# One kernel, one change: the small matmuls of a first loop put one by one between its wide ones

## The chip, the cores and the metric

The kernel runs on one core of one Trainium2 chip. The metric is the device time of one execution in microseconds (us), lower is better. TensorE is called PE in the profile, VectorE DVE, ScalarE ACT, GpSimd POOL; SP is the engine whose queue issues the DMAs.

## The reference

One layer of a decoder trunk on x of 2048 rows by 1024 columns, with one conditioning vector c: a modulated norm, a gated short convolution, a residual and a last norm.

```python
def reference(x, c, ..., final_g, l0_ada_w, l0_ada_b, l0_w_in, l0_conv_w, l0_conv_b, l0_w_out):
    shift, scale, gate = split(silu(c) @ ada_w + ada_b, 3)
    h = rmsnorm(x) * (1.0 + scale) + shift            # (2048, 1024)
    u, gc, gb, z = split(h @ w_in, 4)                 # w_in: 1024 x 8192
    conv = causal_conv3(gc * u, conv_w)               # per channel, width 3
    y = (gb * (conv + conv_b) * silu(z)) @ w_out      # w_out: 2048 x 1024
    return rmsnorm(x + gate * y, final_g)
```

## The kernel before, in words

**The big product.** h @ w_in is done by a scheme with seven products in place of eight (the "Pair" class): h and w_in are cut into 2x2 blocks, and sums of blocks are multiplied. Each operand is split in two parts, a rounded one (hi) made by ACT and the rest (lo) made by DVE, and each product is three passes of PE: lo x hi, hi x hi, hi x lo (`PASSES`). A product of one pair is 12 wide matmuls (128x512 out): four contraction tiles by three passes. The operands on the side of h are called by the number of the product: 1 and 2 are the blocks of h of the first 512 rows; 5, 6, 7 and 4 are the sums T1, T2, T3 and T4; 3 is a block of the second 512 rows (`b22`).

**The first loop.** Nothing of h exists at the start. Rows come in chunks of 512 (`x0`, then `x1`): four tiles each, loaded, squared and summed by ACT (`norm_x`, line 110, whose scratch tile `sq` comes from the pool `raw` of four buffers), a root on POOL, scaled by DVE (line 133). For each of the eight contraction tiles k the loop makes shift and scale of that tile, of silu(c) and the weights `ada` (line 181: part of the sum on DVE; line 192: the other part and the sum over partitions by matmuls of one column on PE, here "mods"; lines 193 and 194 copy the two results out), transposes the four tiles of x0 on PE (line 139), applies shift and scale on ACT (`make_h`, line 144), splits, and runs 18 wide matmuls (line 471: products 1 and 2 of six pairs that are kept in six of the eight PSUM banks). Then it does the four transposes and `make_h` for x1, and DVE makes T1 and T2. So a step is, on PE: 8 transposes, 10 mod matmuls, 18 wide. Weights of a step (`raw`, loaded by `load_early`, split to `we`) come through the same pool `raw`.

**After the loop** come the small conv parameters (`make_conv`, whose 16 tiny transposes are line 237), then T3, T4 and all the splits of operands 7, 5, 4 and 3, and then 436 products (line 294), pair by pair, in the order 1, 6, 7, 5, 2, 4, 3; a few side jobs (`make_second`: the same for the other 1024 rows) run between them. At the end y @ w_out (line 646) and the last norm.

**Order.** Each engine works its own queue in order. The order in a queue is set by a scheduler when the program is built, from the order of the code and from when a tile's buffer comes free; DMAs are issued in order by SP. The lines where work stands in the code are printed below, with what calls them.

Of the kernel before, what the change touches and what calls it, by code (L numbers as in the profile page):

```python
# [13 lines left out]
P = 128  # L14
# [4 lines left out]
def trunk_kernel(ctx: ExitStack, tc: tile.TileContext, x, c, final_g, ada_w, ada_b,  # L19
# [47 lines left out]
    def raw(name="raw"):  # L67
        return rawp.tile([P, D], F32, name=name, tag="raw")
# [52 lines left out]
    def load_x(ci):  # L121

        xs = []
        for t in range(ci * ST, (ci + 1) * ST):
            a = op("xn", F32)
            nc.sync.dma_start(a.rearrange("p h n -> p (h n)"), x[t * P:(t + 1) * P, :])
            xs.append(a)
        return xs

    def norm_x(a):  # L130

        scratch = raw("sq").rearrange("p (h n) -> p h n", h=2)
        nc.vector.tensor_scalar_mul(a, a, rstd(square_sum(a, scratch)))

    def turn_x(xns, k):

        tp = bank()
        for t, a in enumerate(xns):
            nc.tensor.transpose(tp[:, t * P:(t + 1) * P], a[:, k // KH, k % KH * P:(k % KH + 1) * P], ident)  # L139
        return tp  # L140

    def make_h(a, tp, k):

# [16 lines left out]
    def mod_start(k):  # L160

        m = sp.tile([P, 2, MC], F32, name="mod", tag="sp")
        nc.vector.memset(m, 0.0)
        nc.sync.dma_start(m[0:1], ada_b.rearrange("(o t n) -> o t n", o=1, t=3)[:, 0:2, k * P:k * P + MC])
        return m

# [28 lines left out]

    def make_gate():

# [133 lines left out]
    class Pair:  # L331


        def __init__(self, hf, g):
            self.g, self.mx = g, mixer(hf, g)
            self.ps = {}

        def target(self, p):

# [26 lines left out]
        def take(self, p, ps):  # L366
            mx, b = self.mx, self.g % 2
            if p == 1:
                self.keep_p1(el("u")[:, :CH])
            elif p == 6:  # L370
                nc.vector.tensor_add(self.u, ps, self.u)
            elif p == 7:
# [7 lines left out]
            elif p == 5:  # L380
# [29 lines left out]
    warm_up(early[-1].ps["A"], ones, 28)  # L410
    x0 = load_x(0)
    mods = [mod_start(k) for k in range(0, KD, 2)]

    def load_early(k):
        r = raw()[:, :2 * EU * P]
# [2 lines left out]
                              w_view[:, k, q, 0:EU, :])  # L418
        return r

    def split_early(r):
        hi, lo = [wp.tile([P, 2 * EU * P], F32R, name="we", tag="w") for _ in range(2)]
        split(r, hi, lo, nc.vector)
        return hi, lo

    def half_block(n):

        ts = [op("hr", F32) for _ in range(2)]
        return [ts[k // 2][:, k % 2] for k in range(KH)]

    ada = {0: load_ada(0)}
    we = {k: load_early(k) for k in range(2)}
    for a in x0:
        norm_x(a)
    ada[2] = load_ada(2)
    x1 = load_x(1)
    h0, h1 = [], []
    bops = {1: [], 2: [], 6: []}
    keep = {}

    def kept(e, name):
# [5 lines left out]
        keep["n"] = keep.get("n", 0) + 1  # L447
        return keep["t"][:, 1 - keep["n"] % 2]

    t2 = []  # L450
    for k in range(KD):
        if k % 2 == 0:
            mod_sum(mods[k // 2], ada[k][:2])
            if 0 < k < KD - 2:
                ada[k + 2] = load_ada(k + 2)
            for i in (k + 2, k + 3):
                if i < KD:
                    we[i] = load_early(i)
        mod_turn(mods[k // 2], ada[k // 2 * 2][2:], k)
        tp = turn_x(x0, k)  # L460
        if k % KH == 0:
            h0 += half_block("h0")
        make_h(h0[k], tp, k)
        t = op("b")
        nc.vector.tensor_copy(t[:, 0], h0[k])  # L465
        nc.vector.tensor_sub(t[:, 1], h0[k], t[:, 0].bitcast(F32))
        bops[1 if k < KH else 2].append(t)
        w = split_early(we.pop(k))
        for n, (i, m) in enumerate(PASSES):
            for e, pr in enumerate(early):  # L470
                nc.tensor.matmul(pr.ps["A"], lhsT=w[i][:, e * P:(e + 1) * P], rhs=t[:, m],  # L471
                                 start=k == 0 and n == 0, stop=k % KH == KH - 1 and n == 2, skip_group_check=True)
        if k == KH - 1:
            for e, pr in enumerate(early):
                pr.keep_p1(kept(e, "p1"), nc.scalar.copy if e % 2 else nc.vector.tensor_copy)
        if k == 0:
            for a in x1:
                norm_x(a)
        if k % KH == 0:
            h1 += half_block("h1")  # L480
        make_h(h1[k], turn_x(x1, k), k)
        if k < KH:
            nc.vector.tensor_sub(h0[k], h1[k], h0[k])
        else:
            t2.append(sp.tile([P, CH], F32, name="t2", tag="sp"))
            nc.vector.tensor_sub(t2[-1], h1[k], h0[k - KH])
            bops[6].append(split_op(t2[-1]))
    for e, pr in enumerate(early):
        pr.take_c11(kept(e, "c11"))
    make_conv()  # L490
    t1, b21, b12, b22 = h0[:KH], h0[KH:], h1[:KH], h1[KH:]
    for k in range(KH):
        nc.vector.tensor_sub(b12[k], b22[k], b12[k])
    bops[7] = [split_op(a) for a in b12]
    bops[5] = [split_op(a) for a in t1]
    for k in range(KH):
        nc.vector.tensor_sub(b21[k], b21[k], t2[k])
    bops[4] = [split_op(a) for a in b21]
    bops[3] = [split_op(a) for a in b22]


    def make_second():
# [58 lines left out]
            yield  # L561


    work = [(0, g + d, p) for g in range(0, 2 * EU, 2) for p in ORDER if p not in (1, 2) for d in range(2)]
# [144 lines left out]
```

## Time and profile before

| | |
|---|---|
| median of 3 runs (lowest to highest) | 1677.51 us (1677.24 to 1679.03) |
| the profiled execution's own time | 1677.48 us |
| its span, first to last instruction | 1675.7 us |
| mean granted clock of PE, 1.0 = full | 0.982 |
| PE busy | 1635.2 us, 98% |
| DVE busy | 1039.4 us, 62% |
| ACT busy | 529.1 us, 32% |

The time of a run is the span and 1.78 us around it. The granted clock is 1.0 at 2.4 GHz and 0.5 at 1.2 GHz; values between are averages. In the profile a float32 matmul of the mods (128x1) is two records of weight load and matmul, a wide matmul and a transpose are one.

### The profile page before, as it was taken

The page shows a single profiled execution, that of the slowest core. Times are in us where ns is not written, and L with a number is a line of the kernel's source. Part 1 is how long each engine was busy: PE and PEld are TensorE (multiplying, and loading weights), DVE is VectorE, ACT ScalarE, POOL GpSimd, SP SyncE. Part 2 cuts the span into 40 slices and gives each one's busy share as a digit, 9 for nine tenths or more (in the row PEclk, how much of TensorE's full clock was granted, in tenths as well). Part 3 has the DMA queues.
Part 4 walks back from the last instruction along what each step waited for, and adds up shares of the span by engine and source line. Part 5 has one row for each costly group of instructions (what it writes and reads, how often), then busy time and mean ns, then how long its engine had stood idle before and what let it go on. Part 6 is the DMA issues. An engine that isn't in the chain of part 4 may idle for free.

```text
span 1675.7 us, 19351 instructions
## 1 busy us (share of the span) xinstructions
PE 1635.2 (98%) x7276; PEld 1351.4 (81%) x7276; DVE 1039.4 (62%) x1602; ACT 529.1 (32%) x881; POOL 150.9 (9%) x230
## 2 busy tenths in 40 slices
PE   6969999999999999999999999999999999999997
PEld 6758888888888878888888888888888888888886
DVE  5568786767787886666766766666666642233331
ACT  4342344443433333333333333333333421111110
POOL 2000120100011011001000000010100100000000
PEclk7879999999999999999999999999999999999999
DMA  8323334334555532752222222222224643333320
GB/s 286 117 82 93 103 95 129 97 121 149 165 176 176 177 125 82 284 181 63 70 76 76 64 63 63 78 74 69 64 70 122 199 144 101 101 101 101 98 85 31
DMA packets 213103, 190.58 MB, mean 114 GB/s; under 512 B 7425, under 2 KB 181513, under 8 KB 213010
## 3 DMA queue, kind: packets, MB, share of 16 engines
q1 hardware_dynamic: 213010, 189.35, 35.9%
q8 instruction: 57, 0.93, 0.2%
q14 instruction: 36, 0.29, 0.1%
HBM read 144.75 MB, written 44.56 MB: 113 GB/s over the span
## 4 chain that ended last, share of the span: by engine, by line
PE 77%; issue 16%; DVE 4%; DMA 2%; POOL 1%; ACT 0%; SPq 0%; DVEq 0%; POOLq 0%; ACTq 0%
PE ps L294 67%; PE ps L646 5%; PE ps L471 2%; PE ps L192 1%; DMA raw<-in_l_w_in_dram 1%; DVE b L148 1%; PE ps L139 1%; DVE w L148 1%; DMA xn<-in_x_dram 0%; POOL rs L118 0%; DVE gate_m L210 0%; POOL t L317 0%; DMA ada<-in_l_ada_w_dram 0%; DVE mod L181 0%; ACT hr L144 0%
## 5 line engine op out<-in xcount | busy, mean ns | idle before, releaser
L294 PE MATMUL ps<-b,w 128*128 128x512 f32 x5232 | 1194.2, 390 | 14.8 <-DVE w L148 13.7
L294 PEld LDWEIGHTS ps<-b,w 128*128 128x128 f32 x5232 | 982.4, 188 | 219.8 <-issue 14.1
L147 ACT CAST w<-raw 128x512 fp32r<-128x512 f32 x244 | 151.7, 622 | 383.0 <-PE ps L294 302.5
L147 ACT CAST w<-s 128x512 fp32r<-128x512 f32 x192 | 118.7, 619 | 200.2 <-PE ps L294 191.5
L646 PE MATMUL ps<-wo,ye 128*128 128x512 f32 x768 | 180.7, 394 | 0.0
L646 PE MATMUL ps<-wo,yw 128*128 128x512 f32 x768 | 176.9, 389 | 0.0
L148 DVE TENSOR_TENSOR w<-s,w 128x512 fp32r<-128x512 f32 x192 | 132.8, 692 | 68.6 <-ACT w L147 68.2
L646 PEld LDWEIGHTS ps<-wo,ye 128*128 128x128 f32 x768 | 144.2, 188 | 34.0
L148 DVE TENSOR_TENSOR w<-raw,w 128x512 fp32r<-128x512 f32 x244 | 167.2, 686 | 4.8 <-ACT w L147 4.6
L646 PEld LDWEIGHTS ps<-wo,yw 128*128 128x128 f32 x768 | 144.2, 188 | 30.3
L659 DVE TENSOR_TENSOR a<-ps,gate 128x512 f32<-128x512 f32 x32 | 22.0, 691 | 191.8 <-PE ps L646 191.7
L316 DVE SCALAR_TENSOR_TENSOR t<-v,cpar,t 128x512 f32<-128x512 f32 x128 | 95.6, 747 | 40.1 <-ACT t L314 39.2
L110 ACT ACTIVATE sq<-xa 128x1024 f32<-128x1024 f32 x16 | 17.0, 1061 | 273.8 <-DVE xa L660 251.2
L312 POOL COPY v<-v 128x2 f32<-128x2 f32 x32 | 20.0, 625 | 740.1 <-DVE v L364 618.9
L318 DVE TENSOR_TENSOR t<-t,gb 128x512 f32<-128x512 f32 x64 | 44.3, 692 | 53.0 <-POOL t L317 53.0
L269 DVE TENSOR_TENSOR s<-raw 128x512 f32<-128x512 f32 x64 | 44.0, 688 | 48.3 <-DMA raw<-in_l_w_in_dram 48.2
L393 DVE TENSOR_TENSOR u<-ps,u 128x512 f32<-128x512 f32 x58 | 39.9, 688 | 39.8 <-PE ps L294 39.8
L353 ACT COPY u<-ps 128x512 f32<-128x512 f32 x58 | 34.0, 586 | 91.9 <-PE ps L294 91.9
L314 ACT ACTIVATE t<-v,cpar 128x512 f32<-128x512 f32 x64 | 52.0, 815 | 5.0 <-DVE v L400 4.3
L471 PE MATMUL ps<-b,we 128*128 128x512 f32 x144 | 45.5, 483 | 5.7 <-DVE b L465 5.7
L317 POOL TENSOR_TENSOR t<-t,sz 128x512 f32<-128x512 f32 x29 | 40.2, 1387 | 115.6 <-DVE t L316 95.2
L317 POOL TENSOR_TENSOR t<-t,u 128x512 f32<-128x512 f32 x29 | 39.4, 1359 | 118.5 <-issue 79.1
(97 smaller groups left out, 948.5 us busy)
## 6 DMA issues: line engine op xcount, KB each, us to landing
raw<-in_l_w_in_dram SPq DMA_DIRECT2D x128, 512.0 KB, 4.3
y_d<-t SPq DMA_DIRECT2D x64, 256.0 KB, 2.4
yr<-y_d SPq DMA_DIRECT2D x32, 512.0 KB, 4.7
op_d<-b SPq DMA_DIRECT2D x28, 512.0 KB, 3.5
b<-op_d SPq DMA_DIRECT2D x28, 512.0 KB, 9.5
xn<-in_x_dram SPq DMA_DIRECT2D x16, 512.0 KB, 4.8
ada<-in_l_ada_w_dram SPq DMA_DIRECT2D x32, 256.0 KB, 4.7
raw<-in_l_w_out_dram SPq DMA_DIRECT2D x16, 512.0 KB, 4.7
```

What stands on the lines that cost most here:

```text
L147: nc.scalar.copy(hi, src)
L148: eng.tensor_sub(lo, src, hi.bitcast(F32))
L269: nc.vector.tensor_add(d, a21, a22)
L294: nc.tensor.matmul(ps, lhsT=w[:, i, k * P:(k + 1) * P], rhs=b[k][:, m], start=first and k == 0 and n == 0, stop=k == KH - 1 and n == 2, sk ...
L314: nc.scalar.activation(t, v[:, 2:], AF.Identity, bias=cpar[:, j, 3:4], scale=cpar[:, j, 2:3])
L316: nc.vector.scalar_tensor_tensor(t, v[:, w:CH + w], cpar[:, j, w:w + 1], t, ALU.mult, ALU.add)
L317: nc.gpsimd.tensor_mul(t, t, self.sz[ci])
L318: nc.vector.tensor_mul(t, t, self.gb[ci])
L353: (eng or nc.scalar.copy)(a, self.ps["A"])
L393: nc.vector.tensor_add(self.u, ps, self.u)
L471: nc.tensor.matmul(pr.ps["A"], lhsT=w[i][:, e * P:(e + 1) * P], rhs=t[:, m], start=k == 0 and n == 0, stop=k % KH == KH - 1 and n == 2, sk ...
L646: nc.tensor.matmul(ps, lhsT=a, rhs=b, start=j == 0 and n == 0, stop=j == NJ - 1 and n == 2)
```

## The change

Five things change, all but one of them in the first loop and around it.

1. **The loop is staggered.** In step k the transposes of tile k+1 (x0), from k = 4 on those of two tiles of x1, and the mods of tile k+2 are generators of which one matmul is taken after each wide one. Before the loop come the mods of tiles 0 and 1 and the transposes of tile 0. Two more rows of warm-up matmuls (16 and 8) stand there.
2. **More of the modulation on DVE.** Of four tiles of `ada` DVE sums three, not two (two for the first pair of tiles): 22 sums of 128x512, not 16, and 20 + 36 mod matmuls on PE, not 80.
3. **The sums T3, T4 and the split of `b22`** leave the gap ahead of the products and come after the first operands: T3 ahead of product 0, T4 behind the first, `b22` behind the third. The six first pairs take the products in the order 6, 5, 7, 4, 3. T1 and T2 are split in the loop.
4. **Loads.** Four weight tiles `raw` are asked for before `norm_x` (two before), `x1` in the loop, the conv parameters at the start (in another pool).
5. **The rounded part of h** is made by ACT (line 150), not by DVE (line 465), and the `mod` tiles are cleared by POOL.

```diff
-        nc.vector.memset(m, 0.0)
+        nc.gpsimd.memset(m, 0.0)
...
                 nc.tensor.matmul(ps[:, t:t + 1], lhsT=a, rhs=b, start=n == 0, stop=n == len(todo) - 1)
+                if (t, n) != (1, len(todo) - 1):
+                    yield
...
-            r = raw("conv")
+            r = op("conv", F32).rearrange("p h n -> p (h n)")
...
+    ON_DVE = {0: KD // AR // 2}
+    def sum_mod(k):
+        mod_sum(mods[k], ada[k][:ON_DVE.get(k, KD // AR - 1)])
...
+    def turn_h0(k):
+        tp = bank()
+        for t in range(ST):
+            turn_one(tp, x0, k, t)
+            if t < ST - 1:
+                yield
+        if k % KH == 0:
+            h0.extend(half_block())
+        make_h(h0[k], tp, k)
+        bops[1 if k < KH else 2].append(split_op(h0[k]))
+        split_early(k)
+        yield
...
+    for k in range(2):
+        we[k] = load_early(k)
+    ada[2] = load_ada(2)
+    for k in range(2, 4):
+        we[k] = load_early(k)
+    for a in x0:
+        norm_x(a)
+    sum_mod(0)
+    warm_up(early[-1].ps["A"], ones, 16)
+    for k in range(2):
+        run_all(turn_mod(k))
+    run_all(turn_h0(0))
...
+        jobs = []
+        if k + 1 < KD:
+            jobs.append(turn_h0(k + 1))
+        if k >= KH:
+            jobs += [turn_h1(2 * (k - KH) + i) for i in range(2)]
+        if k + 2 < KD:
+            jobs.append(turn_mod(k + 2))
...
         for n, (i, m) in enumerate(PASSES):
             for e, pr in enumerate(early):
-                nc.tensor.matmul(pr.ps["A"], lhsT=w[i][:, e * P:(e + 1) * P], rhs=t[:, m],
+                nc.tensor.matmul(pr.ps["A"], lhsT=wk[k][i][:, e * P:(e + 1) * P], rhs=b[:, m],
                                  start=k == 0 and n == 0, stop=k % KH == KH - 1 and n == 2, skip_group_check=True)
+                while jobs and next(jobs[0], StopIteration) is StopIteration:
+                    jobs.pop(0)
...
+    make_t3()
     second = {}
     for n, (hf, g, p) in enumerate(work):
         prepare(n + AHEAD)
+        if n == 1:
+            make_t4()
+        if n == 3:
+            make_b22()
```

What the scheduler made of it, engine by engine. First **PE, in the middle of the loop** (`xn` is a tile of x, `ada` and `mod` belong to the mods, `b` and `we` are the operands of a wide matmul). Before, one whole step:

```order
L139 MATMUL ps<-ident,xn 128x128 x8
L192 MATMUL ps<-sc,ada 128x1 x4
L192 MATMUL ps<-ones,mod 128x1
L192 MATMUL ps<-sc,ada 128x1 x4
L192 MATMUL ps<-ones,mod 128x1
L471 MATMUL ps<-b,we 128x512 x18
```

and now, a piece where the fifth step passes into the sixth:

```order
L195 MATMUL ps<-sc,ada 128x1
L542 MATMUL ps<-b,we 128x512
L195 MATMUL ps<-ones,mod 128x1
L542 MATMUL ps<-b,we 128x512
L143 MATMUL ps<-ident,xn 128x128
L542 MATMUL ps<-b,we 128x512
```

A block of small matmuls ahead of 18 wide ones has become one small after each wide. Not all of it: the transposes of tiles 2, 3 and 4 and the mods of tiles 3 and 4 still stand in blocks, between the wide ones of steps 0 and 1 and of steps 1 and 2.

Then **ACT, from its first work to the first operand of the loop** (`sq` is the scratch of the squares of x0, `we` the weights' rounded parts, `shift` and `scale1` what comes of the mods, `hr` is h). Before:

```order
L110 ACTIVATE sq_177,ss_178<-xn_139 128x1024
L110 ACTIVATE sq_185,ss_186<-xn_141 128x1024
L110 ACTIVATE sq_193,ss_194<-xn_143 128x1024
L110 ACTIVATE sq_201,ss_202<-xn_145 128x1024
L193 COPY shift_99<-ps_239 128x1
L194 ACTIVATE scale1_98<-ps_239 128x1
L147 CAST we_263<-raw_171 128x768
L147 CAST we_348<-raw_174 128x768
L144 ACTIVATE hr_257<-ps_252,shift_99,scale1_98 128x512
```

and now:

```order
L198 COPY shift_99<-ps_284 128x1
L199 ACTIVATE scale1_98<-ps_284 128x1
L150 CAST we_308<-raw_195 128x768
L150 CAST we_362<-raw_198 128x768
L110 ACTIVATE sq_219,ss_220<-xn_139 128x1024
L110 ACTIVATE sq_227,ss_228<-xn_141 128x1024
L110 ACTIVATE sq_235,ss_236<-xn_143 128x1024
L110 ACTIVATE sq_243,ss_244<-xn_145 128x1024
L150 CAST we_423<-raw_213 128x768
L147 ACTIVATE hr_302<-ps_297,shift_99,scale1_98 128x512
```

The four squares of x0, which were the first thing that ACT did, now stand behind the mods of two tiles and behind the split of the first two weight tiles: all four buffers of `raw` are taken by weights, and a scratch tile must wait for one.

Last **DVE, where the loop ends and the products begin** (`s` are sums of weights, `w` the weights' rest parts, `b` with `hr` the rest parts of T1, T3, T4 and `b22`, `t` is T2, `keep` takes a product out of PSUM). Before:

```order
L269 TENSOR_TENSOR s_872<-raw 128x512
L273 TENSOR_TENSOR s_874<-s_872,raw 128x512
L276 TENSOR_TENSOR raw<-raw 128x512
L148 TENSOR_TENSOR b<-hr,b 128x512 x16
L148 TENSOR_TENSOR w<-s_863,w 128x512
```

and now:

```order
L151 TENSOR_TENSOR b<-t_788,b 128x512
L556 TENSOR_TENSOR hr<-hr 128x512 x2
L151 TENSOR_TENSOR w<-raw,w 128x512
L377 TENSOR_TENSOR keep<-ps,keep 128x512
L151 TENSOR_TENSOR b<-hr,b 128x512 x4
L151 TENSOR_TENSOR w<-raw,w 128x512
L561 TENSOR_TENSOR hr<-hr,t_737 128x512
L561 TENSOR_TENSOR hr<-hr,t_752 128x512
L561 TENSOR_TENSOR hr<-hr,t_773 128x512
L151 TENSOR_TENSOR b<-hr,b 128x512 x3
```

The row of 16 rest parts is gone from ahead of the weights' first rest part; four of them are made in the loop, and the others stand between the takes of the first products.

## Rows read from the trace of the kernel before

**Rows 1.** The page: PE's total, and the granted clock in 40 slices.

```profile
PE 1635.2 (98%) x7276; PEld 1351.4 (81%) x7276; DVE 1039.4 (62%) x1602; ACT 529.1 (32%) x881; POOL 150.9 (9%) x230
...
PEclk7879999999999999999999999999999999999999
```

**Rows 2.** Windows of 10 us: length, then PE, PEld, DVE, ACT, POOL busy, clock, DMA.

```profile
100.00:110.00 10.00, 1.81 (x8) 1.15 (x7) 9.53 (x17) 9.29 (x19) 0.00 (x0) 0.84 0.25 69
110.00:120.00 10.00, 4.50 (x11) 3.56 (x12) 9.57 (x16) 5.35 (x10) 0.00 (x0) 0.50 0.34 107
120.00:130.00 10.00, 10.00 (x44) 8.23 (x43) 6.26 (x10) 2.49 (x4) 0.00 (x0) 0.97 0.76 210
130.00:140.00 10.00, 10.00 (x46) 8.26 (x45) 8.73 (x15) 1.87 (x3) 0.19 (x1) 1.00 0.29 84
```

**Rows 3.** Chain that ended last, 0 to 135 us: start, us, what.

```profile
10.11 0.47 SPq L173
...
11.14 5.40 DMA ada<-in_l_ada_w_dram
...
16.58 3.59 PE ps L192 x16
...
26.42 6.89 PE ps L471 x18
...
48.56 0.79 ACT hr L144
...
49.39 2.39 PE ps L192 x20
51.78 5.81 PE ps L471 x18
57.59 0.45 PE ps L139 x4
...
105.12 9.50 DVE b L148 x16
...
115.50 19.67 PE ps L294 x75
```

**Rows 4.** Timeline, 0 to 60 us: start, us, engine, instruction.

```profile
5.06 1.06 ACT L110 ACTIVATE sq<-xn 128x1024 f32<-128x1024 f32 x1 [2.52 <-DMA xn<-in_x_dram]
...
6.33 1.06 ACT L110 ACTIVATE sq<-xn 128x1024 f32<-128x1024 f32 x1
...
11.31 0.57 POOL L118 TENSOR_TENSOR rs<-ms,nhalf 128x1 f32<-128x1 f32 x1
...
14.55 0.99 PE L192 MATMUL ps<-sc,ada 128*128 128x1 f32 x4 [5.36 <-DMA ada<-in_l_ada_w_dram]
15.00 2.74 DVE L133 TENSOR_SCALAR xn<-xn,rs 128x1024 f32<-128x1024 f32 x4
...
20.32 1.56 ACT L147 CAST we<-raw 128x768 fp32r<-128x768 f32 x2
...
21.18 1.83 DVE L148 TENSOR_TENSOR we<-raw,we 128x768 fp32r<-128x768 f32 x2 [3.44 <-ACT we L147]
...
22.93 3.11 DVE L181 SCALAR_TENSOR_TENSOR mod<-ada,sc,mod 128x512 f32<-128x512 f32 x4
```

**Rows 5.** Timeline of PE among the products, 225 to 330 us.

```profile
246.21 5.74 PE L294 MATMUL ps<-b,w 128*128 128x512 f32 x24
...
252.14 5.71 PE L294 MATMUL ps<-b,w 128*128 128x512 f32 x24
...
275.82 8.44 PE L294 MATMUL ps<-b,w 128*128 128x512 f32 x36
```

**Rows 6.** Windows of 2 us in the loop, columns as in rows 2.

```profile
52.00:54.00 2.00, 2.00 (x7) 1.56 (x6) 0.49 (x1) 0.05 (x1) 0.00 (x0) 0.57 0.03 8
...
78.00:80.00 2.00, 1.51 (x14) 1.27 (x13) 1.68 (x4) 1.39 (x2) 0.00 (x0) 1.00 0.09 24
80.00:82.00 2.00, 2.00 (x15) 1.86 (x15) 1.74 (x4) 0.74 (x3) 0.00 (x0) 1.00 0.84 244
```

More of the change, by code (lines that the diff above doesn't have):

```diff
@@ L137, in turn_x, with turn_one @@
         tp = bank()
-        for t, a in enumerate(xns):
-            nc.tensor.transpose(tp[:, t * P:(t + 1) * P], a[:, k // KH, k % KH * P:(k % KH + 1) * P], ident)
-        return tp
+        for t in range(ST):
+            turn_one(tp, xns, k, t)
+        return tp
+    def turn_one(tp, xns, k, t):
+        nc.tensor.transpose(tp[:, t * P:(t + 1) * P], xns[t][:, k // KH, k % KH * P:(k % KH + 1) * P], ident)
     def make_h(a, tp, k):
@@ L335, in __init__ @@
             self.g, self.mx = g, mixer(hf, g)
-            self.ps = {}
+            self.ps, self.c22 = {}, None
         def target(self, p):
@@ L371, in take @@
                 nc.vector.tensor_add(self.u, ps, self.u)
-            elif p == 7:
+            elif p in (7, 5) and self.c22 is None:
                 t = el("gb" if b else "v")
@@ L379, in take @@
                 nc.vector.tensor_add(self.c22, ps, self.u)
-            elif p == 5:
+            elif p in (7, 5):
                 nc.vector.tensor_add(self.c22, ps, self.c22)
@@ L409, in trunk_kernel @@
         pr.target(1)
-    warm_up(early[-1].ps["A"], ones, 28)
-    x0 = load_x(0)
-    mods = [mod_start(k) for k in range(0, KD, 2)]
     def load_early(k):
@@ L419, in load_early, with split_early, half_block @@
         return r
-    def split_early(r):
+    def split_early(k):
         hi, lo = [wp.tile([P, 2 * EU * P], F32R, name="we", tag="w") for _ in range(2)]
-        split(r, hi, lo, nc.vector)
-        return hi, lo
-    def half_block(n):
+        split(we.pop(k), hi, lo, nc.vector)
+        wk[k] = hi, lo
+    def half_block():
         ts = [op("hr", F32) for _ in range(2)]
         return [ts[k // 2][:, k % 2] for k in range(KH)]
[L431 to L438, printed above, removed]
     keep = {}
@@ L448, in kept @@
         return keep["t"][:, 1 - keep["n"] % 2]
-    t2 = []
-    for k in range(KD):
[L452 to L468, printed above, removed]
+    h0, h1, t2 = [], [], []
@@ new lines, in trunk_kernel, with turn_mod @@
+    bops = {1: [], 2: [], 3: [], 4: [], 5: [], 6: [], 7: []}
+    ada, we, wk, mods = {}, {}, {}, {}
+    ON_DVE = {0: KD // AR // 2}
+    def sum_mod(k):
+        mod_sum(mods[k], ada[k][:ON_DVE.get(k, KD // AR - 1)])
+    def turn_mod(k):
+        k2 = k // 2 * 2
+        yield from mod_turn(mods[k2], ada[k2][ON_DVE.get(k2, KD // AR - 1):], k)
+    def turn_h0(k):
+        tp = bank()
+        for t in range(ST):
+            turn_one(tp, x0, k, t)
[6 more added lines that the diff above has]
+        split_early(k)
+        yield
@@ new lines, in turn_h1 @@
+    def turn_h1(k):
+        tp = bank()
+        for t in range(ST):
+            turn_one(tp, x1, k, t)
+            if t < ST - 1:
+                yield
+        if k % KH == 0:
+            h1.extend(half_block())
+        make_h(h1[k], tp, k)
+        if k < KH:
+            nc.vector.tensor_sub(h0[k], h1[k], h0[k])
+            bops[5].append(split_op(h0[k]))
+        else:
+            t2.append(el("t2")[:, :CH])
+            nc.vector.tensor_sub(t2[-1], h1[k], h0[k - KH])
+            bops[6].append(split_op(t2[-1]))
+        yield
@@ new lines, in run_all @@
+    def run_all(job):
+        for _ in job:
+            pass
+    warm_up(early[-1].ps["A"], ones, 28)
+    x0 = load_x(0)
+    make_conv()
+    for k in range(0, KD, 2):
+        mods[k] = mod_start(k)
+    ada[0] = load_ada(0)
+    for k in range(2):
[9 more added lines that the diff above has]
+        run_all(turn_mod(k))
@@ new lines, in trunk_kernel @@
+    run_all(turn_h0(0))
+    warm_up(early[-1].ps["A"], ones, 8)
+    sum_mod(2)
+    x1 = None
+    for k in range(KD):
+        if k == 0:
+            ada[4] = load_ada(4)
+            x1 = load_x(1)
+            we[4] = load_early(4)
+        elif k == 1:
+            we[5] = load_early(5)
+            ada[6] = load_ada(6)
+        elif k == 2:
+            we[6] = load_early(6)
+            we[7] = load_early(7)
+        jobs = []
[5 more added lines that the diff above has]
+            jobs.append(turn_mod(k + 2))
+        b = bops[1 if k < KH else 2][k % KH]
+        if k == 1:
+            sum_mod(4)
+        if k == 3:
+            for a in x1:
+                norm_x(a)
+            sum_mod(6)
@@ L473, in trunk_kernel @@
+        for j in jobs:
+            run_all(j)
         if k == KH - 1:
@@ L475, in trunk_kernel, with make_t3, make_t4, make_b22 @@
                 pr.keep_p1(kept(e, "p1"), nc.scalar.copy if e % 2 else nc.vector.tensor_copy)
[L476 to L487, printed above, removed]
     for e, pr in enumerate(early):
         pr.take_c11(kept(e, "c11"))
[L490 to L499, printed above, removed]
+    def make_t3():
+        for k in range(KH):
+            nc.vector.tensor_sub(h1[k], h1[KH + k], h1[k])
+            bops[7].append(split_op(h1[k]))
+    def make_t4():
+        for k in range(KH):
+            nc.vector.tensor_sub(h0[KH + k], h0[KH + k], t2[k])
+            bops[4].append(split_op(h0[KH + k]))
+    def make_b22():
+        for k in range(KH):
+            bops[3].append(split_op(h1[KH + k]))
     def make_second():
@@ L561, in begin_out @@
             yield
-    work = [(0, g + d, p) for g in range(0, 2 * EU, 2) for p in ORDER if p not in (1, 2) for d in range(2)]
+    work = [(0, g + d, p) for g in range(0, 2 * EU, 2) for p in (6, 5, 7, 4, 3) for d in range(2)]
     work += [(0, g, p) for g in range(2 * EU, NG) for p in ORDER]
```

## The prediction, written before the changed kernel ran

> **What bounds the kernel now.** I read the page first: PE is busy for 98% of the span and its granted clock falls below full only in the first three of 40 slices, the first 126 us [rows 1]. So the rest is the matmuls themselves, and only the start can give something. Then windows: at 100 us PE all but stops, while DVE is busy 9.53 of 10 us [rows 2]. The chain says why: the first loop's wide matmuls begin at 26.42 us, their last end by 101.8 (1.81 us into the window at 100), and the products begin at 115.50, behind 16 rest parts on DVE of 9.50 us [rows 2, 3]. From 115.50 on PE doesn't stop. What the change is worth is how much earlier than 115.50 the products begin, and whether they then run without waits.
>
> Inside the loop the chain repeats each step: 18 wide matmuls (5.81 us), 0.45 of transposes, 0.79 of ACT's h, 2.39 for 20 passes of mods [rows 3]. The wide ones alone would take less at full clock: among the products 36 of them take 8.44 us and 24 take 5.74, so one takes 0.225, and 18 take 4.05 [rows 5]. The rest is the clock: from 49.39 to 51.78 us PE runs only mods [rows 3], and the wide ones behind them get a mean clock of 0.57 at 52 to 54 [rows 6].
>
> **The sum: when does the loop begin?** Later than now; this is the part that speaks against the change. The four squares were ACT's first work at 5.06 us [rows 4]; now they wait for a scratch buffer behind two weight splits, and these stand behind the mods of tiles 0 and 1.
> - Mods: before, the last `ada` load landed at 16.54 (11.14 and 5.40), and 16 passes took 3.59 us, to 20.17; a pass is 0.224 at the half clock of that stretch [rows 3]. Now 40 passes, not 20: 20 more are 4.5 us. PE had waited 1.0 us inside the first tile's mods (15.54 to 16.58), which the second tile fills [rows 3, 4]. So 20.2 + 4.5 - 1.0 = 23.7. If the longer warm-up keeps the clock full, a pass is 0.12 (2.39 for 20) and some 2.5 us less.
> - Weights: ACT's split 0.78 (1.56 for two), DVE's rest part 0.92 (1.83 for two) [rows 4]: the first scratch is free at 25.4, the second rest part done at 26.3.
> - DVE then does six sums (the change adds two here) of 0.78, 4.7 us, to 31.0, and four scalings of x0, 2.74, to 33.8 [rows 4]. The squares, 1.27 apart (5.06 to 6.33), end at 30.5, the last root about 1 us later (POOL's longer step is 0.57) [rows 4]: DVE is later, so it sets the start.
> - The last of the transposes, h (0.79), its rounded part (at most another 0.79) [rows 3], and handing over: 2.2, so 36.0.
> - Four small loads of the conv parameters are issued ahead of `ada`. SP spaced the `ada` loads 0.47 [rows 3], so at most 1.9 us; SP was waiting for landings there, so I take 1.0.
>
> The first wide matmul: 37.0, against 26.42. Bounds 34 and 40.
>
> **How long does it take?** Of 64 transposes 4 are done before; at full clock:
> - 144 wide x 0.225 = 32.4.
> - 60 transposes: among the products 24 wide and 4 transposes take 5.93 (246.21 to 252.14) [rows 5], less 5.40 is 0.53, 0.13 each: 7.8.
> - 36 mod matmuls of two passes of 0.12: 8.6.
> - The first step starts at half clock, as now: 6.89 for 18 wide [rows 3], less 4.05: 2.8.
> - Two joints where the small ones still stand in blocks (steps 0 to 1, 1 to 2): the next operand's ACT work and handing over, 1.0 each: 2.0.
>
> Together 53.6, against 75.4 now; the end is at 90.6. The price of a single small matmul between wide ones isn't in the trace, only four in a row. Half of it (8.2 less) if its weight load hides under the wide one before; 0.2 a pass or transpose if the wide one's load no longer hides (10 more). Nearest is the row with four in a row, which is what I take.
>
> **The handover.** T2 of the last tile needs h, a subtraction and two parts, some 2.7 us; after the last transposes of the last step some ten wide ones (2.3 us) are left, and the first product reaches that tile after nine more (2.0). Hidden. So the products begin at 90.6: 24.9 us earlier. They also begin warm: before, the first 75 took 19.67 us [rows 3], against 16.9 at 0.225: 2.8 more.
>
> **What comes back.** The work of the gap doesn't vanish. T3 and T4 are eight subtractions and eight rest parts, `b22` four: 20 of 0.59 (9.50 for 16), 11.9 us of DVE, now between the first products, where DVE was busy 6.26 and 8.73 of 10 [rows 2]: 5.0 us of room in 20. So 6.9 too much, less what DVE does ahead in the last step. It works in order, so a take of PSUM stands behind parts of `b22`, and product 4, which adds into the bank that product 7 left, waits for it. 0 to 7; I take 3.
>
> **Costed at nothing.** The six more sums in all (4.7 us of DVE) lie beside wide matmuls; without that cover they would cost their length. The conv transposes and the longer warm-up fill PE's wait of 5.36 us for `ada` [rows 4]. ACT makes the rounded part of h while DVE is the busier engine, 62% to 32% [rows 1]. Clearing `mod` on POOL is in nobody's way before 5 us.
>
> The sum: -24.9 - 2.8 + 3.0 = -24.7, a span of 1651.0; with the profiled execution's 1.78 us around it 1652.8, and since its 1677.48 stands 0.03 under the median, 1653.
>
> **The rivals.**
> - *The clock stays at half where small ones alternate (the other side).* From the fourth step on nearly every wide matmul has a small one behind it. That stretch holds 90 wide, 44 transposes and 36 passes, 30.3 us at full clock; at half as much again, and the products' cold start back: 1653 + 30 + 3 = 1686, slower by 0.5%. For it: after a block of mods and transposes the clock fell, as at 52 us [rows 3, 6]. Against: it fell only after stretches without wide matmuls, and at 78 to 82, with the same small ones, it stayed at 1.00 [rows 6]. Lost is the gain when 22 of those 30 us run at half.
>   The Trainium skill (TensorE: Matmul & The Clock Gate, Part 4: PE-mode transpose) says that transposes don't count as busy for the clock gate as other matmuls do; by it this rival would be the forecast if the wide ones between them don't suffice, and the time 1686. The trace agrees at 52 us and not at 80.
> - *The small ones are half price.* The weight loads overlap in general: PEld was busy 8.2 of 10 us under a full PE [rows 2], so there is a little room. 1653 - 8 = 1645.
>   The Trainium skill (TensorE: Matmul & The Clock Gate, Part 2: What happens when you issue a matmul, step 1) says that PE pulls the next weight load ahead under a running matmul; by that rule a single small one costs little more than its own columns, and the time is that of this rival. No run here shows single ones.
> - *DVE is the bound of the loop.* Its work between 37 and 91 us: 12 sums of 0.78, 6 rest parts of weights of 0.92, 4 scalings 2.7, some 41 passes of 0.59, together 42 us of 54. Not full, but in order: a rest part stands behind sums that wait for an `ada` load, and that load is issued only when a buffer of `raw` is free, near 34 us. Two such waits of some 4 us: 1661.
> - *A part of the loop cold:* one or two more falls of the clock at the joints, 2 to 10 us: 1655 to 1663.
>
> **Chances and range.** Forecast 0.62 (its own range 1646 to 1661), half price 0.13, DVE 0.12, a part cold 0.07, half clock 0.06. Faster by over 0.2% (3.4 us, about what can be told from no change) 0.93, same 0.02, slower 0.05. The range: 1643, which takes in half price, to 1668, which takes in the upper price of small ones with the DVE wait, and leaves out the half clock.
>
> **What would show it.** Right: first wide matmul near 37 us, squares of x0 behind 25 us on ACT; the wide ones spread over some 54 us at clock near 1.0 from 42 on; the first product near 91 without a gap; DVE near full in the 25 us after it, with a wait of PE of a few us about the seventh product. Wrong: a clock of 0.5 after 60 us (half clock); a spacing of wide ones with a single small one much under or over 0.35 us (the price); PE waiting on DVE inside steps 1 to 4 (DVE); a first wide matmul outside 34 to 40.

## The result, and the profile after

The changed kernel takes 1656.8 us (median of 4 runs, 1655.86 to 1659.93) against 1677.38 beside it: a ratio of 0.988, 95% interval 0.9862 to 0.9897. Forecast were 1653 us, range 1643 to 1668, faster at 0.93. The gain is 20.6 us, where 24.7 were expected. The profiled execution took 1657.11 us, its span is 1655.3.

The page of the changed kernel, PE's total and the granted clock in 40 slices (answers to [rows 1]):

```profile
PE 1624.2 (98%) x7276; PEld 1341.6 (81%) x7276; DVE 1036.7 (63%) x1596; ACT 532.6 (32%) x889; POOL 163.7 (10%) x234
PEclk7999999999999999999999999999999999999999
```

PE's busy time fell by 11 us, and only the first slice is left below full clock, where there were three. Windows of the changed kernel, columns as in [rows 2]:

```profile
38.00:41.00 3.00, 2.68 (x9) 1.96 (x9) 0.69 (x1) 0.26 (x1) 0.00 (x0) 0.50 0.87 248
42.00:50.00 8.00, 7.68 (x48) 6.71 (x49) 5.06 (x7) 1.86 (x7) 0.00 (x0) 1.00 1.00 366
50.00:90.00 40.00, 37.16 (x209) 30.39 (x208) 31.33 (x48) 28.20 (x53) 6.83 (x8) 1.00 0.42 132
90.00:100.00 10.00, 10.00 (x46) 8.27 (x45) 9.95 (x18) 8.95 (x18) 0.43 (x1) 1.00 0.01 2
100.00:110.00 10.00, 8.66 (x39) 6.84 (x37) 10.00 (x18) 4.25 (x9) 3.09 (x1) 1.00 0.37 99
```

The clock is at 1.00 from 42 us on. The hole of 13.69 us ahead of the products [rows 2, 3] is gone; in its place DVE is full for 20 us, and PE loses 1.34 us in the last window. The timeline of PE in the changed kernel, its three waits within the loop, two stretches of the loop and the way into the products:

```profile
48.24 0.66 PE L143 MATMUL ps<-ident,xn 128*128 128x128 f32 x4 [0.32 <-ACT scale L199]
...
59.09 2.79 PE L542 MATMUL ps<-b,we 128*128 128x512 f32 x11 [1.47 <-DVE b L151]
...
67.94 0.50 PE L542 MATMUL ps<-b,we 128*128 128x512 f32 x1 [1.37 <-DVE keep L359]
...
80.21 0.48 PE L542 MATMUL ps<-b,we 128*128 128x512 f32 x1
80.53 0.28 PE L195 MATMUL ps<-sc,ada 128*128 128x1 f32 x2
80.67 0.47 PE L542 MATMUL ps<-b,we 128*128 128x512 f32 x1
...
82.26 0.48 PE L542 MATMUL ps<-b,we 128*128 128x512 f32 x1
82.58 0.27 PE L143 MATMUL ps<-ident,xn 128*128 128x128 f32 x1
82.60 0.48 PE L542 MATMUL ps<-b,we 128*128 128x512 f32 x1
...
89.82 2.53 PE L542 MATMUL ps<-b,we 128*128 128x512 f32 x10
92.18 16.48 PE L300 MATMUL ps<-b,w 128*128 128x512 f32 x72
110.40 27.48 PE L300 MATMUL ps<-b,w 128*128 128x512 f32 x120 [1.74 <-ACT w L150]
```

Starts are what counts here, since ends overlap. A wide matmul with one mod matmul behind it (two passes) takes 0.46 us, one with a transpose 0.34. The products begin at 92.18, 23.3 us earlier than [rows 3], and the first wait is ahead of the seventh product. What releases it, in the timeline of DVE and ACT of the changed kernel:

```profile
105.96 2.50 DVE L151 TENSOR_TENSOR b<-hr,b 128x512 fp32r<-128x512 f32 x4
108.36 0.69 DVE L385 TENSOR_TENSOR gb<-ps,keep 128x512 f32<-128x512 f32 x1
108.96 0.69 DVE L285 TENSOR_TENSOR s<-raw,s 128x512 f32<-128x512 f32 x1
109.56 0.69 DVE L387 TENSOR_TENSOR v<-ps,v 128x512 f32<-128x512 f32 x1
...
109.74 0.62 ACT L150 CAST w<-s 128x512 fp32r<-128x512 f32 x1 [3.96 <-DVE s L285]
```

The weights' sum `s` stands on DVE behind the four rest parts of `b22`; ACT's cast waits 3.96 us for it, and PE for the cast, which ends at 110.36. The seventh product is a product 4, which writes into the bank that product 7 left, and the take of product 7 (line 387) stands behind the same parts and ends at 110.25, so PE would have been held until then in any case. And the way to the first wide matmul, timeline of ACT, POOL and DVE of the changed kernel (to set beside [rows 4], where the squares began at 5.06):

```profile
25.78 1.56 ACT L150 CAST we<-raw 128x768 fp32r<-128x768 f32 x2
27.63 1.06 ACT L110 ACTIVATE sq<-xn 128x1024 f32<-128x1024 f32 x1 [0.29 <-DVE we L151]
...
32.45 1.32 POOL L118 TENSOR_TENSOR rs<-ms,nhalf 128x1 f32<-128x1 f32 x1
...
34.56 0.93 POOL L118 TENSOR_TENSOR rs<-ms,nhalf 128x1 f32<-128x1 f32 x1
...
35.52 0.75 DVE L133 TENSOR_SCALAR xn<-xn,rs 128x1024 f32<-128x1024 f32 x1 [0.46 <-POOL rs L118]
...
38.30 0.69 DVE L151 TENSOR_TENSOR b<-hr,b 128x512 fp32r<-128x512 f32 x1 [1.16 <-ACT b L150]
```

Squares, roots, scalings, h and its parts hang one behind the other from 27.63 on; the first wide matmul starts at 38.32.

The sum over the spans: products 23.3 us earlier; warm from the start, 72 in 16.48 us, so 75 in 17.2 against 19.67, 2.5 less; waits of PE among the products 5.8 us (1.74, 2.4 and 1.7) against 1.1 before, 4.7 more. Together -21.1; the spans differ by 20.4, and the other 0.7 us stay open. Those waits of the changed kernel (in total, times, longest):

```profile
PE ps L300 <- DVE v L387: 2.4, 2, 1.6
PE ps L300 <- ACT w L150: 1.7, 1, 1.7
PE ps L300 <- DVE gb L385: 1.7, 1, 1.7
```

Lines 385 and 387 are takes of PSUM. The two waits for line 387 (0.84 us at 138.72, 1.61 at 167.87) are those of product 4 for the take of product 7 in the second and third group of pairs; the one for line 385 is at 602 us.

### The profile page after: what moved, and what is told of

Its sections match the earlier page's. It is cut to its first block, busy times and chain, and to the rows that moved or that the text cites. A ratio compares the mean times of both kernels' runs of the same rounds, so it can differ in the third digit from the quotient of the medians.

```text
span 1655.3 us, 19334 instructions
## 1 busy us (share of the span) xinstructions
PE 1624.2 (98%) x7276; PEld 1341.6 (81%) x7276; DVE 1036.7 (63%) x1596; ACT 532.6 (32%) x889; POOL 163.7 (10%) x234
## 4 chain that ended last, share of the span: by engine, by line
PE 71%; issue 18%; DVE 6%; DMA 3%; POOL 2%; SPq 0%; ACT 0%; POOLq 0%; DVEq 0%; ACTq 0%
PE ps L300 63%; PE ps L718 5%; DMA raw<-in_l_w_in_dram 2%; DVE w L151 1%; PE ps L542 1%; POOL rs L118 1%; DMA ada<-in_l_ada_w_dram 1%; PE ps L143 1%; DVE b L151 1%; POOL t L323 1%; POOL ms L116 0%; DVE gate_m L216 0%; DVE t L322 0%; DVE raw L282 0%; DVE s L285 0%
## 5 line engine op out<-in xcount | busy, mean ns | idle before, releaser
L116 POOL TENSOR_SCALAR ms<-ss 128x1 f32<-128x1 f32 x32 | 11.8, 369 | 411.5 <-ACT sq L110 387.1
```

## The experiments

All times are medians. The kernel before, run beside each group, stood at 1676.4 to 1677.2, so the medians can be set side by side within some 1 us. `issue_after(i)` in the diffs queues what its block issues on the engine of `i` behind `i`.

**The gap alone.** The kernel before, with T3, T4 and `b22` moved between the products, and nothing else.

```diff
-    for k in range(KH):
-        nc.vector.tensor_sub(b12[k], b22[k], b12[k])
-    bops[7] = [split_op(a) for a in b12]
...
+        if n == 1:
+            make_t4()
+        if n == 3:
+            make_b22()
```

> The kernel before with only the last part of the change: the sums and splits of T3 stay ahead of the products, T4's go ahead of product 1 and B22's ahead of product 3, the products' order becomes 6, 5, 7, 4, 3; loop, loads and modulation are as before, and T1 is still split behind the loop. Theory A (the parts add: the gap of 9.5 us behind the loop, of which T1's and T3's splits stay, was worth 5 to 7 us, less 2 to 5 us of VectorE's and ScalarE's lateness among the first products): 1671 to 1675. Rival B (the sums only move: TensorE waits among the products for all that the gap lost): 1677 within 2 us. Rival C (the gap was most of the change's gain): 1662 or less.

Measured: 1668.86 us, ratio 0.9953 (0.9938 to 0.9967): 8.4 us less, more than theory A's most and far from C. PE's timeline in it:

```profile
101.48 2.88 PE L294 MATMUL ps<-b,w 128*128 128x512 f32 x12
107.28 5.10 PE L294 MATMUL ps<-b,w 128*128 128x512 f32 x15 [2.91 <-DVE w L148]
```

The products begin right behind the loop, 14.0 us earlier, and 6.4 us come back as waits (7.5 against 1.1). So, if the parts add, 8.4 us of the gain of 20.6 are this part and some 12 the rest of the change. Of that rest, the loads (part 4) and the work moved to ACT and POOL (part 5) were not run by themselves.

**Blocks in place of one by one.** The changed kernel without the two lines that take a small matmul behind each wide one; the small ones of a step stand behind its eighteen wide ones.

```diff
-                while jobs and next(jobs[0], StopIteration) is StopIteration:
-                    jobs.pop(0)
```

> The changed kernel with the same small matmuls, but all those of a step in one block behind its eighteen wide ones instead of one by one. Theory A (what the staggering gives is that the next tile's operand is made while wide matmuls run; the small ones cost TensorE the same in either place): in steps 0 to 3 nothing of later tiles is left to do while h, cast and low part of the next tile are made (about 2 us in a row on ScalarE and VectorE behind the block's four transposes), so TensorE waits about 1 us a step there, less where a block is longer; products begin 2 to 4 us later than in the changed kernel, near 95, and the time is 1658 to 1661. Rival B (one by one is what holds the clock up: blocks of small matmuls let it fall): windows at 0.5 within 45 to 90 us, some 10 us or more lost, 1667 or later. Rival C (the order within a step is worth nothing): products within 1 us of 92.2 and the same time within 2 us.

Measured: 1663.74 us, 6.9 more than the changed kernel; products from 98.80 on. A alone is too small and B's 10 too much: both act. Windows of this run:

```profile
44.00:66.00 22.00, 21.08 (x124) 17.94 (x122) 14.63 (x21) 12.96 (x27) 5.95 (x8) 1.00 0.74 258
68.00:80.00 12.00, 11.19 (x49) 9.01 (x50) 8.00 (x12) 4.86 (x10) 0.00 (x0) 0.78 0.47 132
```

PE waited 1.53 us for DVE's `keep` at 66.8, and the clock stood at half from 68 to 71; the changed kernel waits 1.37 us at the same place and stays at 1.00. It fell again at 78, behind a block of transposes and mods, until 81. The 5.3 us at half clock in 68 to 80 (0.22 of 12, doubled) cost 2.6 us. The rest is mainly the end of that second fall, a start that was 0.7 us later and waits that the changed kernel doesn't have, three of 0.5 us behind the blocks' transposes among them.

**Scratch alone.** The squares of x0 get a scratch tile from the pool of x, not from `raw`.

```diff
-        norm_x(a)
+        norm_x(a, op("sq", F32))
```

> The changed kernel with scratch of its own for the first tiles' squares, and nothing done about the order of ScalarE's queue. Theory A (the squares are late because of their place in ScalarE's queue, behind shift, scale and the casts of two tiles of weights, not because scratch is missing): squares still at 27 to 31 us, first wide matmul within 1 us of 38.3, time within 2 us of the changed kernel. Rival B (it is the scratch, whose buffer the weights' raw tile holds until its low part is done): squares come earlier, first wide at 34 or before.

One run: 1660.67 us. The timeline of its ACT:

```profile
26.93 1.56 ACT L151 CAST we<-raw 128x768 fp32r<-128x768 f32 x2
28.38 1.07 ACT L110 ACTIVATE sq<-xn 128x1024 f32<-128x1024 f32 x1
```

The wait for DVE (0.29 us) is gone, the place in the queue is the same, and the first wide matmul comes at 39.83: 1.5 us later than in the changed kernel, and the time is 3.9 us longer, both outside theory A's bounds, on a single run. But nothing came earlier, so rival B falls: it is the order of ACT's queue. That the scratch of `raw` alone would allow another order wasn't tried.

**Squares first.** The same scratch, and ACT's work on the first tiles queued behind the last square.

```diff
+    with tc.issue_after(sq[-1].ins):
         for k in range(2):
             run_all(turn_mod(k))
         run_all(turn_h0(0))
```

> The changed kernel with the four squares of the first x tiles put at the head of ScalarE's queue, into scratch of their own, ahead of the first tiles' shift, scale and weight casts. Theory A (the first wide matmul at 38.3 is late because squares and roots stand behind the modulation of tiles 0 and 1): x is turned as soon as the modulation is there; shift and scale end near 26, the two casts of weights (1.56 each) stand ahead of h, so the first wide comes at 29 to 32, products begin 6 to 8 us earlier, near 85, and the time is 1648 to 1651. Rival B (the loop then meets loads that come no earlier: weight and ada tiles): the first wide comes as early, but TensorE waits within the loop and 3 to 5 us of it are lost again, 1652 to 1655. Rival C (the roots on GpSimd aren't earlier, since VectorE holds something they need from 19 us on): first wide within 2 us of 38.3, same time.

Measured: 1651.31 us, 5.5 less than the changed kernel, just over A's upper end. Its timeline:

```profile
4.90 1.06 ACT L112 ACTIVATE sq<-xn 128x1024 f32<-128x1024 f32 x1 [2.28 <-DMA xn<-in_x_dram]
...
10.29 0.57 POOL L120 TENSOR_TENSOR rs<-ms,nhalf 128x1 f32<-128x1 f32 x1
...
26.60 0.75 DVE L136 TENSOR_SCALAR xn<-xn,rs 128x1024 f32<-128x1024 f32 x1
...
33.36 0.79 PE L546 MATMUL ps<-b,we 128*128 128x512 f32 x1 [2.17 <-ACT b L153]
```

The roots are there at 10.9, but DVE scales only at 26.60, behind sums that wait for the second `ada` tiles; so the first wide matmul is 5.0 us earlier, not 6 to 9. The loop itself (54.2 us to the products at 87.55) is no longer for it, though its clock came late:

```profile
33.00:44.00 11.00, 10.64 (x33) 8.76 (x34) 3.63 (x5) 2.15 (x5) 0.00 (x0) 0.50 0.98 341
```

**More mods on PE.**

```diff
-    ON_DVE = {0: KD // AR // 2}
+    ON_DVE = {k: KD // AR // 2 for k in range(0, KD, 2)}
```

> The changed kernel with VectorE summing two of the four ada tiles for every pair of columns instead of three for all but the first pair: VectorE is rid of 6 passes of about 0.75 us (some 4.6 us) before 75 us, TensorE gets 24 more 128x1 matmuls of 0.23 us (5.5 us). Theory A (the staggered loop is set by TensorE's own work): loop longer by 4.5 to 5.5 us, products begin near 97, time 1661 to 1663. Rival B (VectorE sets the loop, TensorE only follows): products begin up to 4 us earlier, 1653. Rival C (both are hidden or balance): within 1.5 us of the changed kernel.

Measured: 1660.68 us (1658.68 to 1670.42), 3.9 more; the profiled execution took 1659.47. From the first wide matmul (38.06) to the products (94.11) are 56.05 us against 53.86: 2.2 more, because PE's two waits for DVE inside the loop (1.47 and 1.37 us) are gone. So PE's own work grew by about 5 us, as A has it, and 2.8 of it went into waits that it had anyway: the loop is near balance, between A and C.

**`b22` two products later.**

```diff
-        if n == 3:
+        if n == 5:
             make_b22()
```

> The changed kernel with the four splits of B22 made ahead of product 5 instead of product 3. Theory A (TensorE's 1.74 us ahead of the seventh product is ScalarE's cast of the weights, which waits for the weights' sum, which stands on VectorE behind the four low parts of B22): that wait goes and none takes its place, 1 to 2 us less, 1655 to 1656, which only the trace can tell surely. Rival B (VectorE is full for as long as the first products run, so the wait only moves to a later product): the waits among the first ten products sum to about the same, and the time is the same.

Measured: 1654.65 us (1653.54 to 1655.63), 2.1 less. PE's timeline:

```profile
93.52 43.68 PE L300 MATMUL ps<-b,w 128*128 128x512 f32 x192
```

No wait before 137 us, and the waits among the products sum to 3.0 us, not 5.8. Theory A: the wait doesn't move on. What A leaves out is that the take of product 7 stood behind the same parts; the edit frees both.

**Idle matmuls ahead of the first wide one.** Twenty between the mods and the transposes.

> The changed kernel with 20 of its idle 128x128 matmuls put between the modulation of tiles 0 and 1 and the first transposes, where TensorE waits for 8 us (25.6 to 33.8) and its granted clock is 0.50. Theory A (the clock is at half when the first wide matmul comes because TensorE stood still ahead of it; in the changed kernel and the experiments so far it came back 3.5 to 12 us after the first wide): the first windows of the loop show 1.00 from 38 us on, the first step takes about 6 us instead of 8, products begin 1.5 to 3 us earlier, time 1654 to 1656. Rival B (the wide matmuls of the loop wait for VectorE anyway, 1.47 and 1.37 us, so a faster first step only makes those waits longer): clock as in A, products within 1 us of 92.2, same time. Rival C (the idle matmuls don't raise the clock, and at half clock they run 2 to 3 us past the time at which x is there): products 1 to 3 us later, 1658 to 1660.

Measured: 1656.46 us, no change. The clock was back at 1.00 in 32 to 36 us, and fell again near 37, behind four transposes with waits between (0.50 in 38 to 40): some 3.3 us at half from the first wide matmul on in place of 3.7. The loop took 53.7 us, its waits of 1.49 and 1.32 us stayed. That speaks for B over A, but the clock was hardly better where it mattered, so it decides little.

**The whole start reordered,** and `b22` later. Scalings and first sums first on DVE; biases of later columns and conv loads behind the first `ada` and `raw`; conv turned in the loop.

> The changed kernel with all that stands between the loads and the first wide matmul put in the order of its inputs: squares first on ScalarE, scalings of x first on VectorE, the first ada tiles' sums ahead of the second's, SP's queue with the biases of later columns and the conv loads behind the first ada and weight tiles, the conv turned in the loop; and B22 ahead of product 5. Theory A (the start is a chain of queue places; each of them is worth what it holds up): the first ada tiles land 5 to 6 us earlier, the first wide comes at 25 to 28 us instead of 38.3, products begin 10 to 13 us earlier, about 80 to 82, and with the wait ahead of product seven gone the time is 1641 to 1645. Rival B (the loads set the loop: DMA is at a share of 1.0 in 40 to 50 us already): the first wide comes as early, but TensorE waits for weight, ada and x tiles within the loop, products begin at 84 to 88, time 1646 to 1651. Rival C (at half clock, with no stretch of wide matmuls, the start gains nothing more than the squares alone did): 1650 to 1652.

Measured: 1654.0 us (1652.2 to 1656.76): worse than squares first with less moved. The first wide matmul comes at 22.53, and the products at 92.78. Its windows:

```profile
22.00:34.00 12.00, 11.47 (x35) 9.19 (x36) 6.78 (x10) 2.94 (x6) 0.00 (x0) 0.50 1.07 363
...
50.00:68.00 18.00, 17.13 (x69) 14.24 (x68) 6.05 (x10) 5.16 (x11) 1.51 (x2) 0.50 0.20 59
```

None of the three had foreseen the second row: 18 us at half clock, with PE busy for 17.1 of them. The clock fell at 48.6, behind a wait of 1.99 us that ended at 47.78; then came tiny transposes of the conv and a block of transposes and mods, and the wide matmuls with small ones between them from 55.45 on did not bring it back until 69. PE's waits within the loop sum to 3.7 us (0.83, 1.99, 0.87), and none is released by a load directly, so B is not shown here. From the first wide matmul to the products are 70.25 us, 16.4 more than in the changed kernel; the clock was at half for some 32 us more, which is 16 us of PE's work.

**Eight wide matmuls alone at the head** of steps 0 to 3 of that kernel.

```diff
-                while jobs and next(jobs[0], StopIteration) is StopIteration:
+                while jobs and (k >= KH or n * len(early) + e >= 7) and next(jobs[0], StopIteration) is StopIteration:
```

> The kernel with the whole start reordered (first wide matmul at 22.5, yet products at 92.8, as its clock stood at 0.50 from 22 to 34 and again from 49 to 69 us), with eight wide matmuls alone at the head of steps 0 to 3. Theory A (that start was lost to the clock, which small matmuls between the wide ones kept down after each wait): the stretches at 0.50 last 4 to 6 us instead of 12 to 20, products begin 5 to 9 us earlier, 1645 to 1650. Rival B (the loads set that loop: TensorE's waits for weight and ada tiles only get longer by what the clock gives): products within 2 us of 92.8, 1652 to 1656. Rival C (clock as before, whatever the order): 1654 within 2 us and the same stretches at 0.50.

Measured: 1651.9 us (1648.37 to 1655.1); the profiled execution, at 1648.37, has its products at 87.29 and stretches at half clock of 3 to 7 us. As A says for the clock; but here B shows too: PE waited 5.25 us, up to 44.03, for ACT, which waited 9.04 us, up to 41.81, for the load of a weight tile:

```profile
41.81 0.83 ACT L153 CAST we<-raw 128x768 fp32r<-128x768 f32 x1 [9.04 <-DMA raw<-in_l_w_in_dram]
...
44.03 7.11 PE L555 MATMUL ps<-b,we 128*128 128x512 f32 x18 [5.25 <-ACT b L153]
```

The runs spread over 6.7 us, and the profiled one is the fastest of the four.

**Squares first and `b22` later together,** without and with eight wide ones alone in step 0.

> The two edits that each gained alone, together: squares at the head of ScalarE's queue, and B22 ahead of product 5. Theory A (they act at different places, the first ahead of 38 us, the second at the seventh product, so their gains add: 1656.8 - 1651.3 = 5.5 and 1656.8 - 1654.65 = 2.1): 1648 to 1650. Rival B (VectorE is full from 80 us on, so products that begin earlier wait more): 1651 or more.

> The kernel of the run with both edits, and in step 0 the first eight wide matmuls run alone before the small ones are put between. Theory A (at half clock, wide matmuls with a small one after each hold the clock down: with squares first the step ran interleaved from 33.4 to 41.1 at 0.50, then eight wide alone, and 1.00 came at 45; with B22 later 1.00 came at 51, 11 us after the first wide; in the kernel before, with eighteen in a row, it came within 4 us): the first step's clock is back within 4 to 5 us of the first wide, up to 3 us less, 1645 to 1648. Rival B (when the clock comes back does not hang on the small ones: in the changed kernel itself it came 3.6 us after the first wide, among the small ones): no gain beyond 1 us, 1648 to 1650; or, since the next tile's transposes come later, a wait of 1 us in step 1 and 1649 to 1651.

Measured: 1648.81 us (1647.39 to 1650.35) and 1649.4 (1648.33 to 1649.58). The gains add (theory A of the first). The second is B's by its time. The first one's clock, with small matmuls between from the start:

```profile
32.00:36.00 4.00, 3.50 (x12) 2.69 (x12) 1.51 (x2) 0.98 (x2) 0.00 (x0) 0.50 0.92 287
37.00:60.00 23.00, 20.10 (x115) 17.12 (x115) 15.71 (x22) 12.26 (x27) 4.14 (x7) 1.00 0.80 278
```

Back within 4.5 us of the first wide matmul at 32.49; in the second kernel it took some 6 us. So alternation doesn't always keep the clock down.

**Scalings first, loads as they were.** The second of these, with x's scalings, the conv's copy and the first sums in this order on DVE.

```diff
+    with tc.issue_after(last.ins):
+        turn_conv(convs)
         sum_mod(0)
...
+    with tc.issue_after(sums[3].ins):
         sum_mod(2)
```

> The kernel with both edits and eight wide matmuls alone at the head of step 0, and now x's scalings, the conv's copy and the first ada tiles' sums in that order on VectorE, ahead of the sums of the second ada tiles (in the run with both edits the first scaling stood behind two waits for those tiles, until 26), and the casts of the first two weight tiles ahead of shift and scale; the loads' order is left alone. Theory A (what stands between 26 and 33 us is still only order): first wide matmul at 28 to 30, products begin 2 to 4 us earlier than 86.3, near 83, time 1645 to 1647. Rival B (from here on the loads set the loop, as in the run with the whole start reordered, where earlier first steps only met longer waits): the first wide comes as early, but waits for ada and weight tiles in steps 1 to 3 take it back, products at 85 to 87, time 1648 to 1650. Rival C (TensorE's clock falls in those waits and costs more than the start gains): 1651 or more.

Measured: 1644.82 us (1644.16 to 1649.68), ratio to before 0.9817 (0.9804 to 0.983): the fastest of all, 12 us under the changed kernel. Its timeline:

```profile
11.63 0.75 DVE L136 TENSOR_SCALAR xn<-xn,rs 128x1024 f32<-128x1024 f32 x1 [0.77 <-POOL rs L120]
...
28.98 0.83 ACT L153 CAST we<-raw 128x768 fp32r<-128x768 f32 x1 [1.12 <-DMA raw<-in_l_w_in_dram]
29.71 0.61 ACT L153 CAST b<-hr 128x512 fp32r<-128x512 f32 x1
...
30.38 3.78 PE L557 MATMUL ps<-b,we 128*128 128x512 f32 x8 [3.46 <-ACT b L153]
...
83.41 16.94 PE L310 MATMUL ps<-b,w 128*128 128x512 f32 x74
```

Theory A in the products (83.41) and the time. h's cast now stands behind the cast of the third weight tile, which waits for its load: 1.9 us that are still order.

## Why the prediction was right, and where it was off

**What bounds the kernel.** Right: all of the gain is in the first 115 us and the waits behind them. The stage y @ w_out begins 20.2 us earlier (1294.1), and the spans differ by 20.4.

**The start: 37.0, measured 38.32.** The effect (squares behind 25 us) was forecast, the reason given was wrong: the step "now they wait for a scratch buffer behind two weight splits". With scratch of their own they came as late; queued first they came at 4.90 and the kernel gained 5.5 us. They waited for their place on ACT. Two terms were small. The conv loads, taken at 1.0 (at most 1.9): `ada`'s last wait on PE ended at 18.63, not 16.54, and the mods at 25.62, 1.9 over the 23.7 of that line. And "DVE is later, so it sets the start": POOL's roots took 0.93 to 1.32 us, not 0.57, so DVE waited 0.46 us for the last of them.

**The loop: 53.6, measured 53.86.** Its prices held. Beside 0.225 for the wide one, a single transpose costs 0.12 (0.13 forecast), a mod matmul 0.23 (0.24). *Half price* falls: four in a row and one by one cost about the same. The Trainium skill (TensorE: Matmul & The Clock Gate, Part 2: What happens when you issue a matmul) lets weight loads run ahead under a running matmul; here a single small matmul behind a wide one was no cheaper for it. That the total fits to 0.3 us is partly luck. The cold start was 1.8 us, not 2.8. The two joints, 2.0, cost one wait of 0.32 us. Against these stand two waits for DVE that the sum didn't have, 1.47 us ahead of the third pass of step 2 and 1.37 in the middle of the loop, where DVE takes products out of PSUM: 2.8 us, where *DVE is the bound* had 8.

**Half clock.** In the changed kernel the rival didn't come: 1.00 from 42 us on. But the reason for only 0.06, "it fell only after stretches without wide matmuls", tells when it falls, not whether it comes back among alternating ones: in the reordered kernel it stayed at 0.50 for 18 us. In the changed kernel the waits within the loop, of up to 1.47 us, didn't bring it down. In the run with both edits a wait of 2.58 us didn't either, and in the reordered kernel the clock fell behind one of 1.99.

**What comes back: 3, measured 4.7.** Right place (about the seventh product), within 0 to 7, and the kind was right too: the take of product 7, which product 4 waits for, stood behind the rest parts of `b22` and ended at 110.25. What the prediction didn't have is that the weights' sum stood there as well, and ACT's cast of it came last, at 110.36. Moving the parts freed both: 2.1 us less. Product 4 waited for the take of product 7 twice more, 2.4 us in all, long after `b22`, and one more take held PE for 1.7 us at 602 us; the rule of thumb (6.9 us too much of DVE's work, a part done ahead) had none of these.

**The sum.** -24.9 became -23.3 (start 1.3, loop 0.3), the warm start -2.5 for -2.8, the waits 4.7 for 3.0: 3.6 us of the 4.1 by which the gain fell short. All of these lie inside their bounds.

## What to carry to other kernels

When a change adds work ahead of a first dependent chain, read each in-order queue for what stands ahead of that chain's links: here squares, then scalings, stood behind work that waited for later loads, and putting them first, with `b22` later, was worth 12 us without any less work. At full clock small matmuls between wide ones cost their own time and no more (0.12 and 0.23 us here); the same ones in blocks cost 6.9 us more, in waits and in falls of the clock. So the stretch without wide matmuls, not the small matmul, is what to remove. And where DVE is full, put off what is needed last (`b22`): a weights' sum that stood behind it stopped ACT and PE.

## What the runs showed of the hardware

**How long the clock stays at half behind a wait differs from run to run of nearly the same stream.** From the first wide matmul on, where small ones stood between from the start, it was back within 3.5 to 4.5 us in four profiles (the changed kernel, scratch alone, more mods, both edits) and after some 12 in three (`b22` later, squares first, the reordered start); where eight or eighteen wide ones ran alone first, in 3.5 to 6.1 us in six of six (the kernel before, 5.4, and the gap alone among them). In the three late ones, and in the 18 us of the reordered start, it came back only some 1 us behind a row of eight wide ones alone. That suggests that alternation can hold it down, but seven and six profiles don't settle it, and the medians of with and without in step 0 are alike (1648.81 and 1649.4). Eight us more at half clock are 4 us of PE's work. Executions of one kernel differ as well: those of "more mods on PE" took 1658.68 to 1670.42 us at mean granted clocks of 0.992 and 0.985, and 0.007 of 1660 us is 11.6 us, by this estimate all of that difference. So a gain of 1 or 2 us between two medians here needs the trace beside it. The Trainium skill (TensorE: Matmul & The Clock Gate, Part 4: PE-mode transpose) says that transposes don't count for the clock as other matmuls do: 50 to 90 us of the changed kernel, at 1.00 with a transpose or a mod matmul behind most wide ones, don't show it; the 18 us at 0.50 would fit it, but they hold mods as well as transposes, so no run here tells the two apart.

**POOL's one-column roots mostly take longer beside a busy DVE:** 0.57 us alone (squares first), 0.93 to 1.32 in the changed kernel, while DVE summed and scaled. Not always: in the kernel before, the root at 11.31 took 0.57 us [rows 4] although DVE's sums ran from 11.28 on. The Trainium skill (GPSIMD Engine Reference, 8. Key points) says that POOL shares its SBUF interfaces with DVE, with contention where a DVE instruction has two inputs there or runs in a 2-port mode; the sums have two such inputs, and the changed kernel agrees, the root at 11.31 does not.
